# Weights' second parts by an adding DMA, four sets of parts, no parts kept in DRAM

## The chip, the cores and the metric

The kernel runs on one core of a Trainium2 chip. The metric is the device time of one execution in microseconds (us); the median of three runs before is 2469.33 us. Five engines work in parallel, each through its own queue in order: TensorE (PE, its weight loads PEld), VectorE (DVE), ScalarE (ACT), GpSimd (POOL) and SyncE (SP, which here only issues DMAs). POOL issues DMAs too; the transfers of all of them run on the core's 16 DMA engines.

## What is computed

One encoder layer over two sequences of 1024 tokens by 1024 channels. Each sequence is normalised and projected with w_in (1024 by 8192). A Fourier branch, a two-step long convolution (Hyena) branch and their gates follow; each branch is projected by a 1024 by 1024 matrix, they are merged by sigmoid gates, projected once more, normalised and added to the input.

```python
xn = rmsnorm(x, g_pre)
p = xn @ w_in
fv, fg, hv, hg, mg = jnp.split(p, [...], axis=-1)
fz = jnp.fft.fftn(fz, axes=(1, 3), norm="ortho").real
y_f = (fz * jax.nn.silu(fg)) @ w_fourier_out
...
for n, gate in enumerate((x1, x2)):
    z = gate * long_conv(z, kf[:, n], hyena_d[n])
y_h = (z * jax.nn.silu(hg)) @ w_hyena_out
g_f, g_h = jnp.split(jax.nn.sigmoid(mg + b_merge), 2, axis=-1)
out = (g_f * y_f + g_h * y_h) @ w_out
return x + rmsnorm(out, g_post)
```

All is float32. TensorE is fed with a rounded type (F32R), so each operand is held as two parts: the rounded value h, and the rest l = value - h. A product takes three matmuls (h by h, h by l, l by h).

## The kernel before

The stages, by their place in the span: Fourier branch of both sequences (to about 700 us; from some 200 us on, the filters of the convolutions and most gate sections of the first sequence are worked in between), convolutions of the first sequence (about 760 to 1145) and of the second (1145 to 1710), the rest of the second sequence's gate sections (to 1960, most of it in a form that has its own weights' parts), the output projections `phase_out` (1960 to 2306) and the last projection `last_rows` (to the end). The order on each engine is made when the kernel is built, by a scheduler that estimates durations.

A weight tile [128, 1024] is used in two halves [128, 512], 256 KB each. What becomes of a half:

- `inproj` (line 714) makes the input projections: SP loads the raw half wr (line 729), ACT rounds it into wh (line 171), POOL subtracts, wl = wr - wh (line 181). There are two buffers each of wr, wh and wl. In the convolutions of the first sequence POOL also stores both parts in DRAM (d_w, line 733), and for the second sequence SP loads the two parts from there (line 726), with no rounding and no subtraction. A half feeds 24 matmuls: 4 blocks of 128 rows, 2 halves of the sequence, 3 products.
- `weight` inside `phase_out` (line 1106) does it for the output projections: POOL loads the raw half (line 1113), ACT rounds, DVE subtracts. There are three sets: two in the pool wp, and every third half has one of its own in the pool op. A half feeds 12 matmuls, as each unit of work has half a sequence. There are 4 units, 2 matrices, 8 output tiles and 2 halves: 128 halves. For each output tile a 256 KB gate g is loaded (line 1141), passed through a sigmoid on ACT (line 1143) and multiplied in by DVE; the next unit's operands (sf, sh) are loaded and split meanwhile (lines 1099 and 1103).
- `phase_gates` and `last_rows` take the same two tags wh and wl for two of their parts, split by ACT and DVE.

`split` (line 168) writes h by ACT or DVE and l by POOL or DVE. A tile's buffers are taken in turn; whoever writes a buffer waits until its last reader is done.

Of the kernel before, what the change touches and what calls it, by code (L numbers as in the profile page):

```python
# [9 lines left out]
F32 = mybir.dt.float32  # L10
F32R = mybir.dt.float32r
# [3 lines left out]
MUL, ADD, SUB = ALU.mult, ALU.add, ALU.subtract  # L15

P = 128
D = 1024
L = 1024
# [142 lines left out]
class K:  # L162
# [5 lines left out]
    def split(self, h, l, src, eng="pool", heng="act"):  # L168
# [4 lines left out]
            nc.vector.tensor_copy(h, src)  # L173
        self.left = self.sub(eng, l, src, h)

    def stt(self, eng, out, a, s, b, op0=MUL, op1=ADD):
        self.nc.vector.scalar_tensor_tensor(out, a, s, b, op0=op0, op1=op1)  # L177

# [18 lines left out]
    def setup(self, ctx):  # L197
        tc, nc, a = self.tc, self.nc, self.a
        self.cp = cp = ctx.enter_context(tc.tile_pool(name="cp", bufs=1))
        self.ps = ctx.enter_context(tc.tile_pool(name="ps", bufs=2, space=bass.MemoryType.PSUM))  # L200
        self.dr = ctx.enter_context(tc.tile_pool(name="dr", bufs=1, space=bass.MemoryType.DRAM))

        def ld(name, shape, src, eng=nc.sync):
            t = cp.tile(shape, F32, name=name)
            eng.dma_start(t, src)
            return t
        self.ident = ld("ident", [P, P], a["c_id"], nc.gpsimd)
        self.gpre = ld("gpre", [P, 8], a["g_pre"], nc.gpsimd)
# [12 lines left out]
        self.d_h1 = dt("d_h1", [P, L])  # L221
        self.d_x = [[dt(f"d_x{b}_{k}", [P, L]) for k in range(8)] for b in range(NB)]
        self.d_fz = [[dt(f"d_fz{b}_{k}", [P, L]) for k in range(8)] for b in range(NB)]
        self.d_k = [[dt(f"d_k{n}_{c}", [P, 32 * P]) for c in range(8)] for n in range(2)]
        self.d_g = [{s: [dt(f"d_g{b}_{s}_{k}", [P, L]) for k in range(8)] for s in (0, 4, 5, 6)} for b in range(NB)]
        self.d_w = [[[dt(f"d_w{s}_{k}_{i}", [P, L]) for i in range(2)] for k in range(8)] for s in range(3)]
        self.d_m = [dt(f"d_m{u}", [P, 4, 8, P]) for u in range(2 * NB)]
        self.d_t = [dt(f"d_t{j}", [P, 4, 512]) for j in range(2)]
        self.d_sh = [[dt(f"d_sh{b}_{k}", [P, L]) for k in range(8)] for b in range(NB)]
# [481 lines left out]
            self.xh.append(h)  # L711
            self.xl.append(l)

    def inproj(self, sec, mt, b=None):

        nc, a = self.nc, self.a
        ps = [self.psum("mm", 4, f"pin{n}") for n in range(2)]
        for q in range(2):
            s = slice(512 * q, 512 * q + 512)
            h = self.wp.tile([P, 4, P], F32R, tag="wh", name="wh", bufs=2)  # L720
            l = self.wp.tile([P, 4, P], F32R, tag="wl", name="wl", bufs=2)
            parts = [t.rearrange("p a b -> p (a b)") for t in (h, l)]
            kept = self.d_w[sec - 1][mt] if b is not None else None
            if b:
                for t, k in zip(parts, kept):
                    nc.sync.dma_start(t.bitcast(F32), k[:, s])
            else:
                r = self.wp.tile([P, 512], F32, tag="w", name="wr", bufs=2)
                nc.sync.dma_start(r, a["w_in"][sec, mt][:, s])
                self.split(*parts, r, "pool", "act")  # L730
                if kept:
                    for t, k in zip(parts, kept):
                        nc.gpsimd.dma_start(k[:, s], t.bitcast(F32))
            for n in range(2):
                for kk in range(4):
                    k = 4 * q + kk
                    s = slice(512 * n, 512 * n + 512)
                    self.mm3(ps[n], (h[:, kk], l[:, kk]), (self.xh[k][:, s], self.xl[k][:, s]), k == 0, k == 7)
        return ps

    def conv(self, sec, ct, ws, name, b):
        nc = self.nc
        ps = self.inproj(sec, ct, b)
        out = ws.tile([P, L], F32, tag="u" if sec == 1 else "x", name=name, bufs=1 if sec == 1 else 4)
        w = lambda j: self.wsh[:, ((sec - 1) * 8 + ct) * 3 + j:((sec - 1) * 8 + ct) * 3 + j + 1]
        H = 512
        for n in range(2):
            nc.scalar.activation(out[:, H * n:H * n + H], ps[n], AF.Copy, scale=w(1))
        for o, n, r in ((1, 0, slice(0, H)), (H + 1, 1, slice(0, H - 1))):
            o = out[:, o:o + r.stop]  # L750
            self.stt("dve", o, ps[n][:, r], w(0), o)
        for o, n, r in ((0, 0, slice(1, H)), (H - 1, 1, slice(0, H))):
            o = out[:, o:o + r.stop - r.start]
            self.stt("dve", o, ps[n][:, r], w(2), o)
        return out
# [215 lines left out]
    def phase_gates(self):  # L971
# [3 lines left out]
        tc, nc, a = self.tc, self.nc, self.a  # L975
        wp, b = self.wp, 1
        jobs = [(s, c) for c in range(0, 8, 2) for s in (0, 4, 5, 6) if (s, c) not in self.PLAIN]
        with ExitStack() as es:
            pool = lambda n: es.enter_context(tc.tile_pool(name=n, bufs=1, reuse_waits="tile"))
            gs, gw, gr = pool("gs"), pool("gw"), pool("gr")  # L980
            def prepare(sec, c):


                r = gr.tile([P, 4, 512], F32, tag="raw", name="wraw", bufs=2)
                for i in range(2):
                    nc.gpsimd.dma_start(r[:, 2 * i:2 * i + 2].rearrange("p a b -> p (a b)"), a["w_in"][sec, c + i])
                s = gw.tile([P, 4, 512], F32, tag="sum", name="wsum", bufs=1)
                A = {}

                def parts(n, pool, tags, src, bufs):  # L990
                    h, l = [pool.tile([P, 4, P], F32R, tag=t, name=t, bufs=bufs) for t in tags]
                    self.split(h.rearrange("p a b -> p (a b)"), l.rearrange("p a b -> p (a b)"), src, "dve", "act")
                    A[n] = h, l
                parts("11", wp, ("wh", "wl"), r[:, 0], 2)
                parts("12", wp, ("wh", "wl"), r[:, 1], 2)
# [86 lines left out]
    def phase_out(self):  # L1082
# [6 lines left out]
        with ExitStack() as es:  # L1089
            pool = lambda n: es.enter_context(tc.tile_pool(name=n, bufs=1, reuse_waits="tile"))  # L1090
            bl, sp, oc, sc, op = pool("bl"), pool("sp"), pool("oc"), pool("sc"), pool("op")
            self.nw = 0

            def operand(i, nm, k):

# [10 lines left out]
            def weight(w, dt, q):  # L1106


                own = self.nw % 3 == 2
                self.nw += 1  # L1110
                pool, nb = (op, 1) if own else (wp, 2)
                r = pool.tile([P, 512], F32, tag="w", name="wr", bufs=nb)
                nc.gpsimd.dma_start(r, a[w][dt][:, 512 * q:512 * q + 512])  # L1113
                h = pool.tile([P, 4, P], F32R, tag="wh", name="wh", bufs=nb)
                l = pool.tile([P, 4, P], F32R, tag="wl", name="wl", bufs=nb)
                self.split(h.rearrange("p a b -> p (a b)"), l.rearrange("p a b -> p (a b)"), r, "dve", "act")
                self.weighed, self.weighed2 = self.rounded, self.left
                return h, l

# [118 lines left out]
    def last_rows(self, units, B11, B21, B22, T1, T2, T3, T4, gp, op):  # L1238
# [6 lines left out]
        def prepare(i):  # L1245
# [14 lines left out]
            for n, r, pool, nb in (("11", r0, op, 1), ("12", r1, wp, 2)):  # L1260
                parts(n, r, *[pool.tile([P, 4, P], F32R, tag=t, name=t, bufs=nb) for t in ("wh", "wl")])
# [176 lines left out]
```

## Time and profile before

| what | value |
|---|---|
| three runs, us | 2466.95, 2469.33, 2469.89 |
| span of the profiled execution, us (first to last instruction) | 2468.1 |
| mean granted TensorE clock | 0.994 |
| moved by DMA | 429.39 MB, 174 GB/s in the mean |
| raw halves loaded for the input projections | 136, median 3.1 us to landing |
| raw halves loaded for the output projections | 64 + 64, median 3.9 and 3.8 us to landing |
| parts stored in DRAM, and loaded again | 96 stores (4.0 and 4.9 us), 96 loads (2.9 and 3.7 us) |

The page and the traces give times from the start of the span. Busy times are sums over instructions of one engine; "idle before" is how long that engine stood still ahead of the group, with the releaser that ended most of it. A DMA's time to landing runs from its issue. The DMA share is the mean busy share of the 16 DMA engines. For the profiled execution the page gives the span alone; the median of the runs is 1.2 us above it.

### The profile page before, as it was taken

What the parts mean: (1) busy time and instruction counts of PE and PEld (TensorE: products, weight loads), DVE (VectorE), ACT (ScalarE), POOL (GpSimd) and SP (SyncE); (2) the same over time, 40 slices, a digit from 0 to 9 for tenths busy, and PEclk for the clock granted to TensorE, in tenths of its full rate; (3) what the DMA queues carried; (4) which work ended last, traced back from release to release, by engine and by line L of the source; (5) the groups of instructions that cost most, each with busy time, mean ns of one, the idle gap of its engine ahead of it and who ended that gap; (6) DMA issues with size and microseconds to landing.
All of it is one profiled execution on the core that took longest, in us unless ns stands there. A gap on an engine that the chain in (4) does not pass through costs nothing.

```text
span 2468.1 us, 37202 instructions
## 1 busy us (share of the span) xinstructions
PE 2408.3 (98%) x13196; PEld 2090.7 (85%) x13196; DVE 1947.5 (79%) x3725; ACT 1093.3 (44%) x2041; POOL 498.2 (20%) x516
## 2 busy tenths in 40 slices
PE   6999999999989999999999999999999999999998
PEld 6988888888878988888889888888788888888886
DVE  7687788888888999999889999985565455665677
ACT  5546666666654333334223222333343444544443
POOL 1331222212234333442000000112200012112121
PEclk9999999999999999999999999999999999999999
DMA  7535544444556455545443443435445567776543
GB/s 272 180 128 210 206 163 151 156 160 156 169 184 201 161 176 175 162 161 199 137 145 129 137 144 131 136 129 175 154 162 173 196 201 267 246 244 221 165 168 128
DMA packets 225155, 429.39 MB, mean 174 GB/s; under 512 B 23542, under 2 KB 87255, under 8 KB 224456
## 3 DMA queue, kind: packets, MB, share of 16 engines
q1 hardware_dynamic: 198444, 333.34, 40.6%
q0 software_dynamic: 26336, 93.65, 10.8%
q8 instruction: 104, 1.70, 0.3%
q14 instruction: 83, 0.68, 0.1%
q10 hardware_dynamic: 188, 0.02, 0.0%
HBM read 290.60 MB, written 136.31 MB: 173 GB/s over the span
## 4 chain that ended last, share of the span: by engine, by line
PE 55%; DMA 2%; issue 1%; DVE 1%; POOL 0%; ACT 0%; DVEq 0%; SPq 0%; ACTq 0%; POOLq 0%
PE pin L194 20%; PE pg L194 8%; PE po L194 6%; PE pT L194 6%; PE pyh L194 5%; PE pX L194 5%; PE pyf L194 5%; DMA wr<-in_w_fo 1%; PE tph L785 1%; DMA g<-d_g 1%; DMA wr<-in_w_ho 0%; DVE wl L181 0%; POOL wr L1113 0%; ACT wh L171 0%; POOL wl L181 0%
## 5 line engine op out<-in xcount | busy, mean ns | idle before, releaser
L194 PE MATMUL pin<-xh,wh 128*128 128x512 f32 x1472 | 578.2, 394 | 4.3 <-DVE v L177 2.9
L194 PE MATMUL pin<-xh,wl 128*128 128x512 f32 x1472 | 577.1, 393 | 2.5 <-POOL wl L181 2.5
L194 PE MATMUL pin<-xl,wh 128*128 128x512 f32 x1472 | 578.4, 393 | 0.0
L181 POOL TENSOR_TENSOR wl<-wr,wh 128x512 fp32r<-128x512 f32 x136 | 253.5, 1865 | 1162.8 <-ACT wh L171 1120.3
L194 PEld LDWEIGHTS pin<-xh,wh 128*128 128x128 f32 x1472 | 278.4, 189 | 55.6 <-DVE v L177 3.1
L194 PEld LDWEIGHTS pin<-xh,wl 128*128 128x128 f32 x1472 | 278.3, 189 | 54.0 <-POOL wl L181 3.4
L194 PEld LDWEIGHTS pin<-xl,wh 128*128 128x128 f32 x1472 | 278.5, 189 | 51.5 <-DVE xl L181 0.4
L171 ACT CAST wh<-wr 128x512 fp32r<-128x512 f32 x264 | 162.7, 618 | 304.3 <-PE pin L194 106.8
L194 PE MATMUL pT<-cinv,yh 128*128 128x256 f32 x1024 | 192.1, 282 | 0.0
L194 PEld LDWEIGHTS pT<-cinv,yh 128*128 128x128 f32 x1024 | 164.8, 190 | 9.5 <-ACT yh L171 0.2
L181 DVE TENSOR_TENSOR t<-pX,k 128x1024 f32<-128x1024 f32 x128 | 155.4, 1214 | 9.7 <-PE pX L194 8.7
L181 DVE TENSOR_TENSOR wl<-wr,wh 128x512 fp32r<-128x512 f32 x128 | 87.1, 687 | 92.6 <-ACT wh L171 92.3
L194 PE MATMUL pX<-bh,cfwd 128*128 128x256 f32 x768 | 160.1, 287 | 0.0
L194 PE MATMUL pyf<-sf,wh 128*128 128x512 f32 x512 | 157.7, 389 | 0.0
L194 PE MATMUL pyh<-sh,wh 128*128 128x512 f32 x512 | 157.2, 389 | 0.0
L171 ACT CAST yh<-y 128x512 fp32r<-128x512 f32 x128 | 79.5, 621 | 153.7 <-DVE y L181 120.6
L194 PE MATMUL pT<-cinv,yl 128*128 128x256 f32 x512 | 144.9, 283 | 1.2 <-DVE yl L181 1.2
L171 ACT CAST bh<-b 128x512 fp32r<-128x512 f32 x144 | 88.6, 619 | 119.9 <-DVE b L181 81.5
L181 DVE TENSOR_TENSOR bl<-b,bh 128x512 fp32r<-128x512 f32 x144 | 110.6, 769 | 23.4 <-ACT bh L171 23.4
L194 PEld LDWEIGHTS pX<-bh,cfwd 128*128 128x128 f32 x768 | 125.5, 190 | 3.0
L194 PEld LDWEIGHTS pyf<-sf,wh 128*128 128x128 f32 x512 | 96.0, 188 | 20.3 <-ACT wh L171 0.5
L194 PEld LDWEIGHTS pyh<-sh,wh 128*128 128x128 f32 x512 | 96.1, 188 | 20.0
(350 smaller groups left out, 5322.9 us busy)
## 6 DMA issues: line engine op xcount, KB each, us to landing
k<-d_k SPq DMA_DIRECT2D x128, 512.0 KB, 4.0
wr<-in_w_in SPq DMA_DIRECT2D x136, 256.0 KB, 3.1
d_g<-gt SPq DMA_DIRECT2D x124, 256.0 KB, 2.5
d_k<-kt SPq DMA_DIRECT2D x128, 128.0 KB, 2.2
d_k<-kt SPq DMA_DIRECT2D x64, 256.0 KB, 2.3
wr<-in_w_fo POOLq DMA_DIRECT2D x64, 256.0 KB, 3.9
g<-d_g SPq DMA_DIRECT2D x64, 256.0 KB, 3.8
wr<-in_w_ho POOLq DMA_DIRECT2D x64, 256.0 KB, 3.8
```

The costliest lines, as they stand in the source:

```text
L171: self.rounded = nc.scalar.copy(h, src)
L181: return e.tensor_tensor(out, a, b, op=op)
L194: return self.nc.tensor.matmul(out, lhsT, rhs, start=start, stop=stop, skip_group_check=shared)
L785: nc.tensor.transpose(tp[:, q * P:(q + 1) * P], eo[:, e, q], self.ident)
```

## The change

A new helper makes the two parts. ACT rounds the raw half into h, ACT writes -h into l, and a DMA issued from POOL adds the raw half to l, read from DRAM a second time, where the addition is made by the transfer itself. `inproj` uses it for every half of both sequences, and nothing is stored in d_w or loaded from it; `weight` uses it in the output projections. The tags wh and wl have four buffers in wp, the raw half two; the third set in op is gone. `phase_gates` and `last_rows` keep their own way of splitting and take the four buffers. The memory that the kernel reserves for descriptors of POOL's DMAs is set to 8192.

```diff
+    def parts(self, h, l, r, src):
+
+        nc = self.nc
+        self.rounded = nc.scalar.copy(h, r)
+        nc.scalar.mul(l, h, -1.0)
+        self.left = nc.gpsimd.dma_start(l, src, accum_op=ADD)
...
-    def inproj(self, sec, mt, b=None):
+    def inproj(self, sec, mt):
...
-            h = self.wp.tile([P, 4, P], F32R, tag="wh", name="wh", bufs=2)
-            l = self.wp.tile([P, 4, P], F32R, tag="wl", name="wl", bufs=2)
-            parts = [t.rearrange("p a b -> p (a b)") for t in (h, l)]
-            kept = self.d_w[sec - 1][mt] if b is not None else None
-            if b:
-                for t, k in zip(parts, kept):
-                    nc.sync.dma_start(t.bitcast(F32), k[:, s])
-            else:
-                r = self.wp.tile([P, 512], F32, tag="w", name="wr", bufs=2)
-                nc.sync.dma_start(r, a["w_in"][sec, mt][:, s])
-                self.split(*parts, r, "pool", "act")
-                if kept:
-                    for t, k in zip(parts, kept):
-                        nc.gpsimd.dma_start(k[:, s], t.bitcast(F32))
+            h = self.wp.tile([P, 4, P], F32R, tag="wh", name="wh", bufs=4)
+            l = self.wp.tile([P, 4, P], F32R, tag="wl", name="wl", bufs=4)
+            r = self.wp.tile([P, 512], F32, tag="w", name="wr", bufs=2)
+            src = a["w_in"][sec, mt][:, s]
+            nc.sync.dma_start(r, src)
+            self.parts(*[t.rearrange("p a b -> p (a b)") for t in (h, l)], r, src)
...
-                own = self.nw % 3 == 2
-                self.nw += 1
-                pool, nb = (op, 1) if own else (wp, 2)
-                r = pool.tile([P, 512], F32, tag="w", name="wr", bufs=nb)
-                nc.gpsimd.dma_start(r, a[w][dt][:, 512 * q:512 * q + 512])
-                h = pool.tile([P, 4, P], F32R, tag="wh", name="wh", bufs=nb)
-                l = pool.tile([P, 4, P], F32R, tag="wl", name="wl", bufs=nb)
-                self.split(h.rearrange("p a b -> p (a b)"), l.rearrange("p a b -> p (a b)"), r, "dve", "act")
+                r = wp.tile([P, 512], F32, tag="w", name="wr", bufs=2)
+                src = a[w][dt][:, 512 * q:512 * q + 512]
+                nc.gpsimd.dma_start(r, src)
+                h = wp.tile([P, 4, P], F32R, tag="wh", name="wh", bufs=4)
+                l = wp.tile([P, 4, P], F32R, tag="wl", name="wl", bufs=4)
+                self.parts(h.rearrange("p a b -> p (a b)"), l.rearrange("p a b -> p (a b)"), r, src)
...
-    nc = bacc.Bacc("TRN2", target_bir_lowering=False, num_devices=1)
+    nc = bacc.Bacc("TRN2", target_bir_lowering=False, num_devices=1, dynamic_dma_scratch_size=8192)
```

The order on the engines is new nearly everywhere in detail. Two places carry it. On POOL, in the output projections, before (wr is a raw half; POOL has nothing but these loads there):

```order
L1113 DMA wr_21582<-in_w_ho 128x512
L1113 DMA wr_21611<-in_w_ho 128x512
L1113 DMA wr_21629<-in_w_ho 128x512
L1113 DMA wr_21658<-in_w_ho 128x512
L1113 DMA wr_21676<-in_w_ho 128x512
```

Each load waits for a free buffer, three halves back. The same place with the change (L1108 is the raw load, L181 the adding DMA into wl; the raw half of wl_21505 is wr_21502, and so on, 3 lower):

```order
L181 DMA wl_21505<-in_w_ho 128x512
L1108 DMA wr_21579<-in_w_ho 128x512
L181 DMA wl_21533<-in_w_ho 128x512
L1108 DMA wr_21598<-in_w_ho 128x512
L181 DMA wl_21552<-in_w_ho 128x512
L1108 DMA wr_21628<-in_w_ho 128x512
```

Loads and adding DMAs now alternate: the raw load of the half after the next stands just ahead of a half's adding DMA. On ACT at that place, before (g is the gate with its sigmoid, sf and sh the next unit's operands):

```order
L171 CAST wh_21613<-wr_21611 128x512
L171 CAST wh_21631<-wr_21629 128x512
L171 CAST sf5_21602<-sf5_21602 128x512
L1143 ACTIVATE g_21651<-g_21651,bm_70 128x512
L171 CAST wh_21660<-wr_21658 128x512
L171 CAST wh_21678<-wr_21676 128x512
```

and with the change (L179 rounds, L180 writes the negated part):

```order
L179 CAST wh_21504<-wr_21502 128x512
L1138 ACTIVATE g_21523<-g_21523,bm_70 128x512
L180 ACTIVATE wl_21505<-wh_21504 128x512
L179 CAST wh_21532<-wr_21530 128x512
L180 ACTIVATE wl_21533<-wh_21532 128x512
L179 CAST wh_21551<-wr_21549 128x512
L171 CAST sf0_21521<-sf0_21521 128x512
L1138 ACTIVATE g_21572<-g_21572,bm_70 128x512
L180 ACTIVATE wl_21552<-wh_21551 128x512
```

Each rounding has its negation behind it, for every second half with a gate's sigmoid in between.

More of the change, by code (lines that the diff above doesn't have):

```diff
@@ L225, in setup @@
         self.d_g = [{s: [dt(f"d_g{b}_{s}_{k}", [P, L]) for k in range(8)] for s in (0, 4, 5, 6)} for b in range(NB)]
-        self.d_w = [[[dt(f"d_w{s}_{k}_{i}", [P, L]) for i in range(2)] for k in range(8)] for s in range(3)]
         self.d_m = [dt(f"d_m{u}", [P, 4, 8, P]) for u in range(2 * NB)]
@@ L742, in conv @@
         nc = self.nc
-        ps = self.inproj(sec, ct, b)
+        ps = self.inproj(sec, ct)
         out = ws.tile([P, L], F32, tag="u" if sec == 1 else "x", name=name, bufs=1 if sec == 1 else 4)
@@ L993, in parts @@
                     A[n] = h, l
-                parts("11", wp, ("wh", "wl"), r[:, 0], 2)
-                parts("12", wp, ("wh", "wl"), r[:, 1], 2)
+                parts("11", wp, ("wh", "wl"), r[:, 0], 4)
+                parts("12", wp, ("wh", "wl"), r[:, 1], 4)
                 self.add("dve", s[:, 0:2], r[:, 2].unsqueeze(1).to_broadcast([P, 2, 512]), r[:, 3::-3])
@@ L1091, in phase_out @@
             bl, sp, oc, sc, op = pool("bl"), pool("sp"), pool("oc"), pool("sc"), pool("op")
-            self.nw = 0
             def operand(i, nm, k):
@@ L1259, in xpair @@
                 return t[:, 0], t[:, 1]
-            for n, r, pool, nb in (("11", r0, op, 1), ("12", r1, wp, 2)):
-                parts(n, r, *[pool.tile([P, 4, P], F32R, tag=t, name=t, bufs=nb) for t in ("wh", "wl")])
+            for n, r in (("11", r0), ("12", r1)):
+                parts(n, r, *[wp.tile([P, 4, P], F32R, tag=t, name=t, bufs=4) for t in ("wh", "wl")])
             s13 = xp.tile([P, 2, 512], F32, tag="xl3", name="ms13", bufs=1)
```

## The prediction

> **What bounds the kernel now.** I read the engines' shares first, then windows stage by stage, then who waits for whom, then the DMA queues. The shares and slices of the page:
>
> ```profile
> PE 2408.3 (98%) x13196; PEld 2090.7 (85%) x13196; DVE 1947.5 (79%) x3725; ACT 1093.3 (44%) x2041; POOL 498.2 (20%) x516
> ```
>
> TensorE is the bound, with 2468.1 - 2408.3 = 59.8 us without a matmul in the span. The windows (us from the span's start; length; busy us of PE, PEld, DVE, ACT, POOL; granted clock; DMA share; GB/s) say where:
>
> ```profile
> 200.00:300.00 100.00, 97.26 (x543) 84.60 (x542) 71.49 (x148) 61.22 (x121) 23.51 (x22) 0.98 0.65 233
> 300.00:500.00 200.00, 194.61 (x1046) 168.06 (x1045) 163.36 (x391) 131.82 (x289) 43.72 (x25) 0.98 0.48 156
> 500.00:700.00 200.00, 195.13 (x1038) 167.67 (x1036) 166.47 (x387) 126.33 (x275) 44.17 (x33) 0.99 0.51 165
> 700.00:760.00 60.00, 54.44 (x287) 46.70 (x288) 52.94 (x117) 27.58 (x58) 19.64 (x22) 0.94 0.58 189
> 760.00:1145.00 385.00, 383.84 (x2311) 342.01 (x2311) 372.95 (x642) 140.89 (x237) 148.76 (x131) 1.00 0.50 167
> 1145.00:1645.00 500.00, 500.00 (x2982) 444.21 (x2981) 455.36 (x835) 152.69 (x253) 24.28 (x10) 1.00 0.43 146
> 1710.00:1766.00 56.00, 54.26 (x239) 44.51 (x239) 36.43 (x37) 21.18 (x28) 19.45 (x15) 1.00 0.64 225
> 1960.00:2306.00 346.00, 345.50 (x1522) 284.88 (x1521) 203.76 (x312) 161.41 (x266) 67.31 (x126) 1.00 0.70 235
> ```
>
> From 760 on TensorE hardly stops. The output projections (1960 to 2306) lose 0.5 us, and there the DMA engines are busiest: 0.70 of their time. TensorE's pace stands in the chain of waits (start, us, what):
>
> ```profile
> 1709.97 43.11 PE pin L194 x190
> 1999.90 43.52 PE pyh L194 x192
> ```
>
> A matmul takes 43.52 / 192 = 0.227 us. A weight half feeds 24 matmuls in the input projections (5.44 us) but only 12 in the output projections: **2.72 us** for each of their 128 halves.
>
> **The change, part by part.**
>
> *Subtractions leave POOL and DVE.* Their rows, and the one for DVE's same-shaped split in the convolutions:
>
> ```profile
> L181 POOL TENSOR_TENSOR wl<-wr,wh 128x512 fp32r<-128x512 f32 x136 | 253.5, 1865 | 1162.8 <-ACT wh L171 1120.3 <-PE pft L194 14.5 <-PE pXf L194 10.3
> L181 DVE TENSOR_TENSOR wl<-wr,wh 128x512 fp32r<-128x512 f32 x124 | 84.4, 686 | 80.6 <-ACT wh L171 80.3
> PE pin L194 <- POOL wl L181: 2.5, 2, 1.7
> PE pyh L194 <- DVE wl L181: 0.5, 1, 0.5
> ```
>
> POOL loses 253.5 us and DVE 128 x 0.686 = 88 us, but TensorE waited 2.5 + 0.5 = 3.0 us for them in the whole span. That is all these can give directly: -3 us.
>
> *ACT gains 312 negations* (136 + 48 + 128) and 48 roundings that the second sequence used to skip. The nearest row for a scaled copy of this shape, SBUF to SBUF, is the first; the others stand around it in the output projections:
>
> ```profile
> L1034 ACT ACTIVATE gt<-gt 128x512 f32<-128x512 f32 x24 | 14.9, 633 | 3.5 <-DVE gt L181 3.5
> L171 ACT CAST wh<-wr 128x512 fp32r<-128x512 f32 x124 | 76.4, 620 | 138.1 <-PE pyh L194 46.9 <-PE pyf L194 44.8 <-DMA wr<-in_w_fo 26.9
> L1143 ACT ACTIVATE g<-g,bm 128x512 f32<-128x512 f32 x64 | 46.1, 722 | 39.5 <-DMA g<-d_g 35.8 <-DVE sh L181 2.1 <-DVE wl L181 0.9
> L171 ACT CAST sh<-sh 128x512 fp32r<-128x512 f32 x31 | 19.0, 614 | 0.0
> L1113 POOL DMA_DIRECT2D wr<-in_w_fo x57 | 30.6, 536 | 128.7 <-DVE wl L181 127.7 <-DMA wr<-in_w_fo 0.7
> ```
>
> 312 x 0.633 + 48 x 0.620 = 227 us on an engine that is busy 1093 of 2468. In the output projections 161.4 + 128 x 0.633 = 242 of 346 us: ACT fits, so 0 us, hidden by TensorE's 2.72 us per half; without that cover it would be 128 x 0.633 = 81 us there.
>
> *312 adding DMAs come, 96 stores to DRAM and 96 loads from it go, 48 weight loads come.* In the convolutions of the first sequence (760 to 1145) two stores per half go and one adding DMA comes; in the second (1145 to 1645) two loads become a load and an adding DMA, 48 halves in 500 us at a share of 0.43, which even at two passes grows by 48 x 0.78 / 500 = 0.07. TensorE has 5.44 us per half there, other matmuls in between, and four sets in place of two. I cost these at 0: the matmuls before them hide the landing, and were they gone each half would cost the 5 us or so of one. The eight gate halves in a row at 1710 to 1766 add 8 x 2 x 0.78 = 12.5 us to the 36 us of work that the engines have in those 56 (the 0.78 is worked out below): room enough, and I allow 3 us, twice what TensorE misses there now. What decides is the output projections. Their queues and landings:
>
> ```profile
> q1 hardware_dynamic: 36093, 47.30, 40.6%
> q0 software_dynamic: 10192, 33.56, 28.9%
> DMA to landing us min/median/max: 2.8/3.8/7.7
> d_w<-wl POOLq DMA_DIRECT2D x48, 256.0 KB, 4.9
> 2120.00:2140.00 20.00, 20.00 (x90) 16.57 (x89) 11.85 (x19) 9.11 (x16) 4.31 (x9) 1.00 0.95 320
> ```
>
> POOL's queue q0 moved 33.56 MB, which is 128 transfers of 256 KB, in 28.9% of 346 us = 100 us of all 16 engines: 0.78 us for each. With q1, the engines are busy 0.695 x 346 = 240.5 us (the two queues of instructions add 1 us). Now 128 adding transfers of the same size come on top. No row shows one. Below, an adding transfer costs the engines what a plain load costs, 0.78 us: 241.5 + 100 = 341.5 us of work in a 346 us stage. It would fit with nothing to spare; the fullest window shown reaches 0.95, so 341.5 / 0.95 = 359 us, +13. Above, it costs two passes, as 256 KB stored and then loaded again does: 241.5 + 200 = 441.5 us, so the stage is **+95 us**, and 441.5 / 0.95 = 465 us, +119, if 0.95 is all they reach. I take two passes: the addition needs the 256 KB of weights and the 256 KB that already lie in the tile, so the same engines have twice the bytes to read.
>
> The Trainium skill (Collectives: The Full Stack, section "The bandwidth ceiling: the fold count and why AG ≠ RS ≠ AR") says the same of another program: a DMA that adds is slower than a copy because of its two source reads, both on the read ring, and it gives a measured ratio of 1.93. By that, as an estimate, the stage would be 88 us longer in place of 95; no run here shows it yet.
>
> *The order* on ACT and POOL there, as it is shown with the change: the raw load of half n+2 is asked for just ahead of the adding DMA of half n. Every second negation stands behind a sigmoid that itself waits for the transfer of g (35.8 us in all before), and the adding DMA and the next raw load wait behind it on POOL. A set is free when TensorE ends half n-4 and needed three halves, 8.16 us, later. On the way: 0.62 + 0.61 + 0.72 + 0.63 us on ACT and 0.54 us on POOL, 3.1 us; so the adding DMA may take 5.0 us to land. A store lands in 4.9, a load and a store in turn 3.8 + 4.9 = 8.7. At 8.7 a set goes round in 3.1 + 8.7 + 2.72 = 14.5 us, 3.63 a half: 128 x 0.91 = +116 us. This is the same wait seen from another side, not a second term: full engines make late landings.
>
> Sum: 2468.1 - 3 + 3 + 95 = 2563 us of span. The median of the runs shown, 2469.33, lies 1.2 us above this execution's span: **2564 us**.
>
> **The rivals.**
>
> *Cheap addition.* An adding transfer costs about one load, 0.78 us. For it: a plain 256 KB transfer also reads and writes, and the tile's old content lies in SBUF, not in DRAM. Against it: even so the stage needs 341.5 of 346 us. +13, up to +40 if landings pass 5.0 us in the full windows: 2482 to 2509.
>
> *Latency, not bytes.* The raw halves had three buffers and have two. A buffer comes round in its landing plus the rounding, and two halves last 5.44 us, so a raw load may take 5.44 - 0.62 = 4.8 us. Today's median is 3.8, but the chain of waits shows loads of
>
> ```profile
> 2132.11 6.21 DMA wr<-in_w_fo
> 2218.07 7.54 DMA wr<-in_w_fo
> ```
>
> At 7.7, the slowest, a half takes (7.7 + 0.62) / 2 = 4.16 us: 128 x 1.44 = +184, so 2653. Its mark is a DMA share well below 0.95 while ACT waits for wr.
>
> *Not slower: the engines hide it and DVE runs freer.* If the adding costs no more than a load and the four sets ride over the full windows, the output projections stay at 346 us, and what is left is relief from 200 to 760, where TensorE lacks 2.7 + 5.4 + 4.9 + 5.6 = 18.6 us. For it: DVE's subtraction of one shape takes longer beside POOL's work,
>
> ```profile
> L181 DVE TENSOR_TENSOR bl<-b,bh 128x512 fp32r<-128x512 f32 x144 | 110.6, 769 | 23.4 <-ACT bh L171 23.4
> ```
>
> 769 ns against 686 where POOL computes nothing. Half of the 18.6 us would be -9: 2460. It decides from the point where an adding transfer costs under 0.8 us of the engines and lands within 5.0 us. Against it: ACT, busiest just there (61 to 66%), gets the negations of 60 gate halves before 760, 38 us.
>
> *Not what it says.* The adding DMA may be cut into far smaller pieces than a row. At four times a load's price, 3.1 us, the output projections alone need 241.5 + 400 us, +295, and the input projections fill too: above 2760.
>
> **How the numbers follow.** Two passes 46%, latency 16%, cheap addition 17%, not slower 17%, small pieces 4%. The forecast is that of two passes, 2564; its own range is 2524 (1.6 passes, 241.5 + 160 us) to 2588 (two passes at 0.95). The range for 8 in 10 reaches from 2475, below the cheap addition's time, to 2655, the slowest latency. What a measurement of this kernel tells from no change is about 0.2%, 5 us. The -9 us rival gives faster 10% and, with only part of the relief, the same 7%; the rest, 83%, is slower.
>
> **What would show it.** Right: in the output projections the DMA share goes to 0.9 or more, the stage lasts about 440 us, TensorE waits there for wl from DMA, and everything up to 1960 starts within 10 us of today. A share near 0.7 to 0.8 with a longer stage is the latency rival; a stage of 346 us at any share makes the prediction wrong; so would a loss that lies in the convolutions, where I cost the change at nothing because the sets are ready long before 5.44 us are over.

## The result

The changed kernel takes 2605.64 us (median of 4 runs, 2595.78 to 2610.54) against 2468.14 (4 runs, 2466.22 to 2469.89): 1.0556 times the time before, with a 95% interval of 1.0532 to 1.058. The profiled run took 2608.23 us, its span is 2606.5: 138.4 us more than the 2468.1 before. The page's first part, in the order of the one before:

```profile
PE 2453.9 (94%) x13196; PEld 2102.0 (81%) x13196; DVE 1816.1 (70%) x3597; ACT 1285.3 (49%) x2394; POOL 482.1 (18%) x596
```

TensorE now lacks 152.6 us of its span, before 59.8. So 92.8 of the 138.4 us are time without a matmul; in the other 45.6 the same 13196 matmuls took longer (2453.9 us busy in place of 2408.3). The windows of the changed kernel (same columns; the bounds of the later ones are shifted with the program):

```profile
200.00:300.00 100.00, 93.32 (x473) 79.31 (x472) 38.53 (x79) 47.97 (x92) 14.64 (x22) 0.95 0.80 243
300.00:500.00 200.00, 197.40 (x1072) 170.31 (x1072) 156.37 (x402) 145.02 (x319) 24.01 (x28) 1.00 0.74 197
500.00:700.00 200.00, 192.84 (x1036) 166.11 (x1035) 150.92 (x391) 139.82 (x305) 22.48 (x26) 0.99 0.72 191
700.00:780.00 80.00, 60.99 (x311) 52.63 (x310) 68.28 (x168) 39.94 (x86) 3.46 (x4) 0.81 0.44 128
780.00:1165.00 385.00, 385.00 (x2326) 343.47 (x2325) 361.57 (x650) 164.72 (x281) 68.32 (x56) 1.00 0.55 145
1165.00:1665.00 500.00, 500.00 (x2977) 444.13 (x2976) 455.04 (x839) 210.39 (x356) 52.80 (x58) 1.00 0.57 149
1728.00:1784.00 56.00, 56.00 (x253) 46.55 (x252) 32.89 (x38) 25.82 (x36) 9.37 (x13) 1.00 0.81 243
1971.00:2444.00 473.00, 392.57 (x1550) 297.69 (x1549) 136.81 (x191) 234.92 (x394) 181.81 (x253) 0.95 0.94 246
```

Two stages lost time. The output projections last 473 us in place of 353 and keep the DMA engines busy for 0.94 of it; TensorE's matmuls there take 392.57 us, about 40 more than before, at a granted clock of 0.95 in place of 1.00. Ahead of the convolutions, from 700 to 780, TensorE lacks 19 us. The convolutions (780 to 1665) and the eight gate halves (1728 to 1784) run without a gap.

To compare kernels I take three marks from the views of single tiles: the first matmul of the gates (pg<-xh,wh), the first of the output projections (pyf<-sf,wh) and the start of their last (pyh<-sh,wl). In the rows (count, ns of one, first and last start) they are 1765.8, 1953.5 and 2305.7 us before, and 1783.8, 1971.5 and 2444.1 after:

```profile
L194 PE MATMUL pg<-xh,wh x80: 389/389/389, 1765.8 to 1936.5; 128*128 128x512 f32 x80
L194 PE MATMUL pyf<-sf,wh x512: 388/389/497, 1953.5 to 2262.0; 128*128 128x512 f32 x171
L194 PE MATMUL pyh<-sh,wl x256: 389/389/500, 2000.2 to 2305.7; 128*128 128x512 f32 x128
...
L201 PE MATMUL pg<-xh,wh x80: 389/389/389, 1783.8 to 1954.5; 128*128 128x512 f32 x80
L201 PE MATMUL pyf<-sf,wh x512: 387/389/794, 1971.5 to 2388.8; 128*128 128x512 f32 x171
L201 PE MATMUL pyh<-sh,wl x256: 387/389/740, 2032.9 to 2444.1; 128*128 128x512 f32 x128
```

So 18.0 us are lost ahead of the gates, 120.4 in the output projections (472.6 against 352.2 us) and nothing behind them: 18.0 + 120.4 = 138.4.

Who waits for whom in the output projections of the changed kernel (engine, tile, releaser; total us, times, longest), for TensorE and then for ACT:

```profile
PE pyh L201 <- DMA wl<-in_w_ho: 26.6, 28, 3.6
PE pyf L201 <- DMA wl<-in_w_fo: 25.0, 20, 3.3
PE pyf L201 <- ACT wh L179: 19.1, 10, 5.6
PE pyh L201 <- ACT wh L179: 9.2, 3, 5.2
...
ACT wh L179 <- DMA wr<-in_w_ho: 70.2, 43, 3.9
ACT wh L179 <- DMA wr<-in_w_fo: 69.4, 37, 4.1
ACT g L1138 <- DMA g<-d_g: 62.7, 19, 8.4
```

TensorE waits 51.6 us for adding DMAs and 28.3 us for roundings; ACT waits 139.6 us for raw halves. Most of these waits are for transfers. Their queues in that window (packets, MB, share of 16 engines), and the median landings over the span:

```profile
q0 software_dynamic: 28507, 67.17, 63.1%
q1 hardware_dynamic: 37043, 48.91, 31.0%
...
wr<-in_w_fo POOLq DMA_DIRECT2D x64, 256.0 KB, 5.9
wl<-in_w_fo POOLq DMA_DIRECT2D x64, 256.0 KB, 6.7
```

POOL's queue moved 67.17 MB, as much as 256 transfers of 256 KB (a few of them belong to the last projection), in 63.1% of 473 us = 298 us. If 128 plain ones cost 0.78 us each as before, 198 us are left for 128 adding ones: about 1.55 us each, twice a load. A raw half now lands in 5.9 us, before in 3.8.

### The profile page after: what moved, and what is told of

It is laid out like the page before. It is cut to its first block, busy times and chain, and to the rows that moved or that the text cites. A ratio compares the mean times of both kernels' runs of the same rounds, so it can differ in the third digit from the quotient of the medians.

```text
span 2606.5 us, 37627 instructions
## 1 busy us (share of the span) xinstructions
PE 2453.9 (94%) x13196; PEld 2102.0 (81%) x13196; DVE 1816.1 (70%) x3597; ACT 1285.3 (49%) x2394; POOL 482.1 (18%) x596
## 4 chain that ended last, share of the span: by engine, by line
PE 70%; DMA 14%; issue 7%; DVE 4%; POOL 2%; ACT 2%; SPq 0%; POOLq 0%; DVEq 0%; ACTq 0%
PE pin L201 36%; PE pT L201 7%; PE pX L201 6%; PE pg L201 6%; PE po L201 6%; DMA wr<-in_w_fo 5%; DMA wr<-in_w_ho 4%; PE pXf L201 2%; PE pfv L201 2%; POOL wl L181 1%; PE tph L783 1%; DMA d_g<-gt 1%; POOL wr L1108 1%; PE pft L201 1%; DMA g<-d_g 1%
## 5 line engine op out<-in xcount | busy, mean ns | idle before, releaser
L181 POOL DMA_DIRECT2D wl<-in_w_in x184 | 160.5, 874 | 1321.6 <-ACT wl L180 1097.7
L179 ACT CAST wh<-wr 128x512 fp32r<-128x512 f32 x312 | 193.1, 619 | 419.6 <-PE pin L201 245.0
L180 ACT ACTIVATE wl<-wh 128x512 fp32r<-128x512 f32 x312 | 195.6, 628 | 5.3 <-issue 1.2
L201 PE MATMUL pyf<-sf,wh 128*128 128x512 f32 x512 | 166.5, 412 | 19.1 <-ACT wh L179 19.1
L201 PE MATMUL pyh<-sh,wl 128*128 128x512 f32 x256 | 104.9, 416 | 26.9 <-DMA wl<-in_w_ho 26.6
L201 PE MATMUL pyf<-sf,wl 128*128 128x512 f32 x256 | 106.3, 420 | 25.2 <-DMA wl<-in_w_fo 25.0
```

The costliest lines, as they stand in the source:

```text
L179: self.rounded = nc.scalar.copy(h, r)
L180: nc.scalar.mul(l, h, -1.0)
L181: self.left = nc.gpsimd.dma_start(l, src, accum_op=ADD)
L201: return self.nc.tensor.matmul(out, lhsT, rhs, start=start, stop=stop, skip_group_check=shared)
```

## Experiments

Times without an interval are single profiled runs; the kernel before ran beside them (medians 2467.66 to 2470.48). Stage means the time between the second and third mark.

**The price by itself.** No layer is computed; 48 transfers of 256 KB of each kind, eight buffers in turn:

```diff
+        for i in range(N):
+            nc.gpsimd.dma_start(T[i % 8], src(i))
+        for i in range(N):
+            nc.gpsimd.dma_start(T[i % 8], src(i), accum_op=ADD)
+        for i in range(N):
+            nc.gpsimd.dma_start(T[i % 8], S[i % 8], accum_op=ADD)
+        for i in range(N):
+            nc.sync.dma_start(T[i % 8].bitcast(F32), src(i))
```

> A small kernel that computes nothing of the layer: 48 transfers of 256 KB each of four kinds, eight in flight at a time: plain loads issued from POOL, adding transfers with the weights read from DRAM, adding transfers with the weights read from SBUF, plain loads issued from SP; then the outputs are written. Two-pass theory: a plain load takes 0.75 to 0.8 us of all engines each (48 in 36 to 38 us), an adding one 1.5 to 1.6 (72 to 77 us), the same from SBUF 1.5 or a little less. One-pass theory: adding and plain ones take the same, 36 to 40 us for 48. Small-pieces theory: over 2.5 us each, 120 us or more for 48.

The slices of the page (GB/s in 40 parts of 229 us), then the DMA issues on POOL (busy us, mean ns): adding from SBUF, adding from DRAM, plain.

```profile
GB/s 151 352 391 383 386 385 377 269 205 204 205 204 205 204 204 205 204 204 205 204 204 196 192 189 184 184 184 184 185 192 252 295 398 386 393 404 406 405 406 238
...
L1418 POOL DMA_DIRECT2D t<-s x48 | 41.4, 866 | 25.9 <-DMA t<-s 22.3
L1416 POOL DMA_DIRECT2D t<-in_w_in x48 | 41.8, 1020 | 15.0 <-DMA t<-in_w_in 14.5
L1414 POOL DMA_DIRECT2D t<-in_w_in x48 | 25.6, 541 | 12.7 <-DMA t<-in_w_in 7.0
```

Plain loads run at about 385 GB/s, 262 KB in 0.68 us; adding ones at 204 GB/s, 1.28 us. Both prices are below what was expected; their ratio, 385 / 204.5 = 1.88, is that of two passes. The Trainium skill (Collectives: The Full Stack, "The bandwidth ceiling: the fold count and why AG ≠ RS ≠ AR") has 1.93 for another program, the rate of a collective that copies over that of one that adds, and puts it down to two source reads; this run is near it. The ratio alone does not tell which of the bytes are counted twice.

Three windows of the same run (length, busy us of POOL, granted clock, DMA share, GB/s), of plain loads from POOL, of adding ones from DRAM, and of plain loads from SP:

```profile
10.00:36.00 26.00, 18.20 (x35) 1.00 1.26 385
55.00:92.00 37.00, 24.96 (x29) 1.00 1.13 204
180.00:195.00 15.00, 0.00 (x0) 1.00 1.03 382
```

The share adds up the times of packets, and goes above 1 here. So a share of 0.9 or more in the kernel does not by itself show that the engines could take no more.

**The output projections taken apart.** First, DVE splits there as before, all else as in the change (four sets, two raw buffers):

```diff
-                self.parts(h.rearrange("p a b -> p (a b)"), l.rearrange("p a b -> p (a b)"), r, src)
+                self.split(h.rearrange("p a b -> p (a b)"), l.rearrange("p a b -> p (a b)"), r, "dve", "act")
```

> The changed kernel with the output projections' second parts made by DVE again (four sets, two raw buffers kept), the input projections' by adding DMAs. If the adding transfers' bytes hold up the output projections: that stage falls back to 346 to 350 us and the time to 2486 (2468 + 18, the loss ahead of it, which stays). If two raw buffers in place of three do it: the stage stays above 400 us and the time above 2540.

2518.91 us, ratio 1.0212 (1.019 to 1.0234): the stage takes 377.8 us, 25.6 more than before, with no adding DMA in it. That lies between the two times expected. Its window, and what ACT waits for there:

```profile
1969.90:2347.50 377.60, 362.42 (x1547) 289.97 (x1546) 206.86 (x315) 162.52 (x267) 68.14 (x127) 0.99 0.67 219
...
ACT wh L171 <- DMA wr<-in_w_ho: 104.3, 51, 7.4
ACT wh L171 <- DMA wr<-in_w_fo: 74.9, 45, 5.1
```

The engines are at 0.67 while ACT waits 179 us for raw halves. This is the mark that the prediction gave for its rival "latency, not bytes". Five raw buffers in place of two test it, with DVE's splits and with the adding DMAs:

```diff
+                own = self.nw % 5 > 1
+                self.nw += 1
-                r = wp.tile([P, 512], F32, tag="w", name="wr", bufs=2)
+                r = op.tile([P, 512], F32, tag="wraw", name="wr", bufs=3) if own else wp.tile([P, 512], F32, tag="w", name="wr", bufs=2)
```

> As e1_out_dve (DVE splits in the output projections, four sets), with five raw buffers there in place of two. If e1's 26 us in the output projections were the two raw buffers, the stage from the first pyf to the last pyh matmul falls from 378 to 352 us and the time from 2519 to 2485 to 2493. If they were something else of the four sets' order, it stays at 375.

> The changed kernel with five raw buffers in place of two in the output projections, adding DMAs kept. Two-pass theory: nothing to gain, the stage stays within 10 us of the changed kernel's (about 466 us), the time 2595 to 2612, DMA share 0.95. Latency theory: ACT no longer waits for raw halves, the stage falls by 40 us or more, the time to 2565 or less.

With DVE's splits: 2487.86 us, the stage 352.3 us, as before. So the 25.6 us came from the raw buffers (two here, three before, five now). With the adding DMAs: 2599.49 us, the stage 461.6, only 11.0 less than the change. The two raw buffers are a real limit, but one that the adding DMAs mostly cover. Then, still with five raw buffers and all halves added, SP issues the raw loads, so that POOL's queue holds adding DMAs alone:

```diff
-                nc.gpsimd.dma_start(r, src)
+                nc.sync.dma_start(r, src)
```

> All 128 halves added, five raw buffers, raw loads issued by SP. If bytes bound the stage (441.5 us of engine work by two passes), the order of issue does not matter and the stage stays at 445 to 465 us (461.4 with POOL issuing) at a share of 0.94 to 0.98. If the order on POOL's queue were the bound, it falls below 435 us, which two passes do not allow.

2581.25 us, the stage 441.2 us, and the DMA share is the highest of all these kernels (window, then the queues in it):

```profile
1975.40:2417.40 442.00, 387.61 (x1552) 301.60 (x1551) 134.62 (x190) 231.41 (x391) 110.99 (x129) 0.94 0.98 260
...
q1 hardware_dynamic: 54213, 80.26, 54.1%
q0 software_dynamic: 18432, 34.35, 43.6%
```

Issuing the raw loads from SP was worth 20.4 us (it changes the order and the queue at once), which "the order of issue does not matter" had not allowed; but below 435 us it does not go either, and 0.98 of 442 us is 433 us of packets' time. That the engines could take no more is not shown by this: at the rates of the run of transfers alone the window's bytes would take, as an estimate, 121 x 1.28 us for the adding ones and 83.2 MB / 385 GB/s for the rest, 371 of the 442 us. The queues give both prices in the kernel itself. On q1, 80.26 MB are 306 plain transfers in 0.541 x 442 = 239 us: 0.78 us each. On q0, 34.35 MB are 131 transfers, ten of them plain (five loads of 512 KB of the last projection); 0.436 x 442 - 10 x 0.78 = 185 us for 121 adding transfers: **1.53 us each, 1.96 times a plain one**.

Half as many adding DMAs (DVE splits every second half), five raw buffers, the raw loads once from POOL and once from SP (the line that both have):

```diff
-                self.parts(h.rearrange("p a b -> p (a b)"), l.rearrange("p a b -> p (a b)"), r, src)
+                (self.split(h.rearrange("p a b -> p (a b)"), l.rearrange("p a b -> p (a b)"), r, "dve", "act") if q else
+                 self.parts(h.rearrange("p a b -> p (a b)"), l.rearrange("p a b -> p (a b)"), r, src))
```

> Five raw buffers in the output projections, and there every second half is split by DVE, every other by an adding DMA: 64 adding DMAs in place of 128. Bytes theory: the engines have 247 + 64 x 1.55 = 346 us of work; at 0.94 the stage lasts 352 to 370 us, time 2488 to 2506. If a fixed cost of the mechanism (the order on POOL, the late landings) decides, half of the 109 us of e4 stays: 405 us and 2540.

> As the half-adding kernel with five raw buffers (stage 412 us at a DMA share of 0.85), but the raw loads are issued by SP, so that POOL's queue holds the adding DMAs alone. If the 60 us there came of adding DMAs that stand behind raw loads on POOL, the stage falls to 352 to 375 us at a share of 0.93 or more. If they came of the adding DMA's own landing behind ACT's rounding and negation (5.6 us in the median), or of engines that are already full in bursts, it stays at 400 to 420 us.

2545.58 and 2532.07 us, stages 412.2 and 399.1 us. The windows of the two, and TensorE's waits in the second:

```profile
1969.00:2381.00 412.00, 369.67 (x1548) 296.37 (x1547) 167.66 (x254) 200.75 (x329) 122.77 (x185) 0.97 0.85 239
```

```profile
1968.00:2368.00 400.00, 366.33 (x1553) 295.68 (x1552) 167.13 (x254) 201.36 (x329) 56.90 (x67) 0.97 0.87 246
...
PE pyf L201 <- DMA wl<-in_w_fo: 17.5, 8, 4.1
PE pyh L201 <- DMA wl<-in_w_ho: 15.3, 9, 4.0
```

Bytes alone would give 241.5 + 64 x 1.56 = 341 us of work, which fits into 352. The stage is 47 us longer all the same, at a share of 0.87. So by the terms set for the first of these two runs the bytes lost (352 to 370 us) and the fixed cost of the mechanism won (405 us). Half the adding DMAs leave 60.0 of 109.4 us with POOL issuing the raw loads, and 46.9 of 89.0 with SP: 0.73 us for each added half, against 0.70 with all of them added. A limit of the engines over the stage as a whole, which 64 added halves stay below, would have left next to nothing. What these runs show is a price per added half, and not a point at which the engines fill; the issue from POOL explains 13 us of it.

TensorE waits 32.8 us for the added halves and the granted clock is 0.97. The trace of the second kernel shows in part what holds them up. One case (start, us, instruction, idle time before it and its releaser):

```profile
2183.60 0.72 ACT L1142 ACTIVATE g<-g,bm 128x512 f32<-128x512 f32 x1 [4.47 <-DMA g<-d_g]
2186.93 0.72 ACT L1142 ACTIVATE g<-g,bm 128x512 f32<-128x512 f32 x1 [1.57 <-DMA g<-d_g]
2189.01 0.61 ACT L179 CAST wh<-wr 128x512 fp32r<-128x512 f32 x1
2189.66 0.63 ACT L180 ACTIVATE wl<-wh 128x512 fp32r<-128x512 f32 x1
2190.59 0.88 POOL L181 DMA_DIRECT2D wl<-in_w_fo  x1 [10.29 <-ACT wl L180]
2195.95 0.50 PE L201 MATMUL pyf<-sf,wl 128*128 128x512 f32 x1 [4.06 <-DMA wl<-in_w_fo]
```

ACT stands at two sigmoids until their gates land, then rounds and negates the next half, and its adding DMA lands 5.3 us after its issue, 4.06 us too late. TensorE waits 17 times for an added half here. In 14 of them ACT had waited for a gate between the negation before and the half's own (of all 64 negations, 29 are of this kind); in the other three the adding DMA took 7.6 to 9.6 us to land (median of all 5.8). No run takes the sigmoids out of ACT's way, or gives the added halves more than four sets, so the gates, the landing, the number of sets and engines that are full for a few us at a time are not separated.

The adding DMA replaced by a plain one to the same place, with everything else as in the change, two raw buffers included (wl then holds the raw weights, not the rest):

```diff
-        self.left = nc.gpsimd.dma_start(l, src, accum_op=ADD)
+        self.left = nc.gpsimd.dma_start(l, src) if plain else nc.gpsimd.dma_start(l, src, accum_op=ADD)
```

> The changed kernel with the output projections' adding DMA replaced by a plain DMA of the same 256 KB into the same tile, at the same place in the queues (the second parts are then the raw weights: the product is wrong by that). Every wait, buffer and queue is as in the changed kernel, only the addition is gone. Two-pass theory: the engines have 241.5 + 100 us of work, the stage takes 350 to 375 us and the time is 2490 to 2515. Latency theory (order on POOL, two raw buffers): the stage stays above 420 us and the time above 2560.

2556.26 us, the stage 418.4 us, just under what the latency theory had (above 420) and far from the 350 to 375 of two passes:

```profile
1974.00:2392.00 418.00, 375.42 (x1547) 297.15 (x1546) 136.65 (x191) 234.29 (x393) 135.43 (x253) 0.96 0.88 278
```

So even a second plain transfer in the same place would have cost this stage 66 us (the raw buffers alone made 25.6 with DVE's splits); the addition itself costs 472.6 - 418.4 = 54 us more, in place of the 100 us that its second pass has in the prediction. The plain transfer with five raw buffers and SP's loads was not run, so how much of the 89 us there belongs to the addition is open.

**Ahead of the output projections.** The kernel before, unchanged in how it makes its parts, but with four sets in wp, two raw buffers and the change's descriptor memory (the diff is against the kernel before, its part in the input projections):

```diff
-            h = self.wp.tile([P, 4, P], F32R, tag="wh", name="wh", bufs=2)
-            l = self.wp.tile([P, 4, P], F32R, tag="wl", name="wl", bufs=2)
+            h = self.wp.tile([P, 4, P], F32R, tag="wh", name="wh", bufs=4)
+            l = self.wp.tile([P, 4, P], F32R, tag="wl", name="wl", bufs=4)
```

> The kernel before, splits and stored parts as they were, with only the memory of the change: four sets in wp (none in op), two raw buffers, 8192 for descriptors. If the 18 us ahead of 1960 come from where the four sets lie in memory (the filters' first load, hidr, is then issued some 100 us late in SP's queue), they are here too: the first pX matmul at 770 us in place of 751, and with the output projections' 26 us that e1 showed the time is 2505 to 2520. If they come from the adding DMAs, pX starts at 751 and the time is 2490 to 2496.

2534.45 us. The gates start at 1796.2 us, 30.4 later than before and 12.4 later than with the change: the loss is there, and larger, without a single adding DMA. (The rest is in the output projections: 386.0 us, 33.8 more than before, again with two raw buffers.) What the traces show late in both is the load of the filters' hidden layer, hidr. Its rows before and with the change (the last times are those of the issue on SP):

```profile
L870 SPq DMA_DIRECT2D hidr<-d_h x1: 326/326/326, 204.6 to 204.6; - x1
```

```profile
L868 SPq DMA_DIRECT2D hidr<-d_h x1: 423/423/423, 263.8 to 263.8; - x1
```

In the kernel of this experiment it is issued at 260.2 us. The descriptor memory is not the reason: the next two kernels have it too, and issue this load early. Until the load lands, the filters' work on DVE and ACT cannot start: DVE is busy 38.53 us of 200 to 300, before 71.49. TensorE does gate sections meanwhile; from 700 to 780 it stands still for 19 us. Next, adding DMAs in all input projections but two sets, so that no tile moves, and the output projections as before (the diff is against the change, its part in the input projections):

```diff
-            h = self.wp.tile([P, 4, P], F32R, tag="wh", name="wh", bufs=4)
-            l = self.wp.tile([P, 4, P], F32R, tag="wl", name="wl", bufs=4)
+            h = self.wp.tile([P, 4, P], F32R, tag="wh", name="wh", bufs=2)
+            l = self.wp.tile([P, 4, P], F32R, tag="wl", name="wl", bufs=2)
```

> Adding DMAs in all input projections, but with two sets of parts as before, so that no tile moves in memory; the output projections as before (DVE subtracts, three sets). Theory A (the 18 us lost ahead of 1960 belong to the four sets' memory, and the adding itself costs the input projections nothing): the filters' hidden layer is loaded at about 204 us again, the Fourier branch ends at 712 to 742 us in place of 763, the convolutions of the first sequence start at or before 751 us, the output projections last 352 us, and the whole 2440 to 2470 us. Theory B (the four sets were what hid the adding): with two sets a half's chain (0.62 + 0.63 us on ACT, 0.5 on POOL, 5.0 to land = 6.8 us) has to fit beside one half's 5.44 us of matmuls; up to 1.4 us is lost at each of the 128 halves of the convolutions' projections that no other matmul covers, so the convolutions lengthen by 50 to 180 us: 2510 to 2640 us, with TensorE waiting there for wl from DMA.

2511.37 us, ratio 1.0172 (1.0159 to 1.0186). hidr is early (201.7 us), and still the gates start 34.6 us later than before, at 1800.4. A new first row stands in TensorE's waits over the whole span:

```profile
PE pin L201 <- DMA wl<-in_w_in: 35.6, 24, 4.8
```

Theory B has the wait right, but not its place and size: 19.2 of the 35.6 us fall between 200 and 700, where the gate sections are, and 7.9 between 700 and 1710, where it had the convolutions lengthen by 50 to 180. That the time lies at the low end of its range is luck. The changed kernel has no such row, so four sets do hide the adding there. Then two of the four sets in another pool (wb), the output projections as before:

```diff
+            room = self.rooms[self.ni % len(self.rooms)]
+            self.ni += 1
-            h = self.wp.tile([P, 4, P], F32R, tag="wh", name="wh", bufs=4)
-            l = self.wp.tile([P, 4, P], F32R, tag="wl", name="wl", bufs=4)
+            h = room.tile([P, 4, P], F32R, tag="wh", name="wh", bufs=2)
+            l = room.tile([P, 4, P], F32R, tag="wl", name="wl", bufs=2)
```

> Adding DMAs in all input projections, four sets there, of which two lie in wp and two in the convolutions' own pool, so that hidr is issued as early as before; output projections split by DVE with three sets and three raw buffers, as in the kernel before; 8192 for descriptors. If adding DMAs in the input projections cost TensorE nothing and free DVE and POOL, the filters end 5 to 15 us earlier: 2452 to 2464. If the 18 us come from the adding DMAs after all: 2480 to 2488.

2504.28 us, ratio 1.0143 (1.0126 to 1.016). hidr is issued at 203.4 us again and the Fourier branch's last matmul pXf starts at 711.4 us, before at 742.0; but the gates start at 1764.6, only 1.2 us early, and then lose some 32 us, since their sums are no longer prepared ahead (the first, xsum, at 1773.1 us, before at 1730.3):

```profile
1764.00:1800.00 36.00, 13.88 (x33) 8.27 (x33) 26.29 (x28) 13.19 (x14) 1.66 (x4) 0.59 0.45 160
```

Last, the kernel with DVE's splits and five raw buffers (2487.86 us), with one line changed: one pool opens ahead of another, which gives hidr other memory.

```diff
-            mf, wa, wb, mi = pool("mf"), pool("wa"), pool("wb"), pool("mi")
+            wa, mf, wb, mi = pool("wa"), pool("mf"), pool("wb"), pool("mi")
```

> As the kernel with DVE's splits and five raw buffers in the output projections (2487.86 us; adding DMAs and four sets in the input projections), with one line changed: of the four pools of the main stage, wa is opened ahead of mf, so that the filters' hidden layer hidr lies in other memory and is the seventh DMA of its group on SP, as before, in place of the thirtieth. Theory A (the 18 us ahead of 1960 come from memory that the four sets push about, which makes hidr late): hidr is issued at about 205 us, the Fourier branch ends at 711 to 742 us, the gates start at 1760 to 1767 us, the output projections last 352 us, the whole 2460 to 2472 us: what the adding DMAs save DVE and POOL then shows as at most 8 us. Theory B (the adding DMAs crowd the transfers between 200 and 760 us, whatever hidr does): hidr early, but the gates start at 1775 us or later, the whole 2480 to 2490 us.

2476.93 us, ratio 1.0031 (1.0018 to 1.0044). hidr's row, and the first matmul of the gates:

```profile
L868 SPq DMA_DIRECT2D hidr<-d_h x1: 327/327/327, 202.7 to 202.7; - x1
...
L201 PE MATMUL pg<-xh,wh x80: 389/389/389, 1766.6 to 1938.9; 128*128 128x512 f32 x80
```

The gates start 0.8 us later than before, in place of 15.0 for that kernel without the line. Theory A holds for where the loss comes from: tiles that the four sets moved in memory, and hidr is the one whose load the traces show late. (The line moves the other tiles of the two pools as well.) The total is 5 us above its range, and the relief it allowed for did not come. This is the best version with adding DMAs that ran; it is still slower than the kernel before, by 8.4 us of span: 3.6 by the start of the output projections and 4.8 in them, which no run explains.

## Why the prediction was right, and where it was not

- **The price of an adding transfer, and the place where it is paid: right.** It was taken at 2 x 0.78 = 1.56 us and measured at 1.53 in the kernel, 1.28 against 0.68 alone. The output projections have 120.4 of the 138.4 us.
- **That full engines set the time there: not shown.** Predicted were 441.5 us of work; the changed kernel's window has 0.94 x 473 = 445 us of packets' time, the one with the highest share 433. But 64 added halves, which leave the engines at 0.87, cost 46.9 us, and 128 cost 89.0. In these two kernels the loss goes with the number of adding DMAs, also where their bytes leave room.
- **The stage: +95 predicted, +120.4 measured.** The step that fails is "the same wait seen from another side, not a second term: full engines make late landings". Late landings come without full engines: at a share of 0.87 the adding DMAs still take 5.8 us (median), where the prediction allows 5.0. By the prediction's own sum for a set's round, the 6.7 us to landing of the row above give 3.1 + 6.7 + 2.72 = 12.5 us, 3.13 a half and, as an estimate, +52 us, with no wait for a gate in it. By the experiments 89.0 us remain with five raw buffers and a queue of its own for the adding DMAs (441.2 - 352.2), 20.4 us came from raw loads and adding DMAs together on POOL, 11.0 from two raw buffers. The three parts come from kernels changed one after the other; in another order they would share out differently, as 25.6 against 11.0 us for the raw buffers shows. So +95 against 89.0, and the +119 with engines at 0.95 against 120.4, are near for a reason that the runs do not bear out, and in that part luck. The measured 2605.64 us lie above the range of the two-pass theory itself (2524 to 2588), inside the range for 8 in 10.
- **"Everything up to 1960 starts within 10 us of today": wrong, 18.0 us.** The 18 us stand at nothing in the sum. The prediction asked what waits for added halves, and not what four sets in wp do to the memory of other tiles. One load then stood some 25 places later on SP, 59 us later in time. It did not follow hidr, whose issue the build's order would have shown.
- **Convolutions and gate halves at nothing: right, for the reason given.** TensorE is busy 385.00 of 385, 500.00 of 500 and 56.00 of 56 us there, with the engines at 0.55, 0.57 and 0.81. With two sets the cover was gone and 35.6 us appeared. The 3 us allowed for the gate halves and the 3 us credited for subtractions both came to about nothing.
- **ACT hidden: only half shown.** 312 negations took 195.6 us (628 ns each, 633 taken), and ACT was not full (234.92 of 473 us). But ACT's order is not free: in the second half-adding kernel 14 of TensorE's 17 waits for an added half have a wait of ACT for a gate ahead of them. How much time that costs was not measured by a run.
- **The rivals.** *Latency* was real: 25.6 us alone for the raw buffers, not the 184 that every load at its slowest would make, and some part of the 89.0 us that no run tells. *Cheap addition* would not have saved the kernel as it is: with a plain second load the stage still grew by 66 us, where the prediction had 13 to 40. *Not slower*: DVE did run freer (the 144 subtractions of the row that the prediction shows, bl<-b,bh, take 709 ns in place of 769; the Fourier branch is 30.6 us earlier with two sets in wb), but the convolutions behind it began only 5.6 us earlier, the gates 1.2, and no version came out faster for it. *Small pieces* fell with the first experiment.

The median came out 41.6 us above the 2564 forecast: 18.0 ahead of the stage and 120.4 - 95 = 25.4 in it, less some 2 us, since this median lies 0.9 us below the profiled execution's span, where the forecast had put it about 1 above.

## What to carry to other kernels

Work moved from an engine into an adding DMA is paid for with two transfers' worth of DMA time, so count it against the fullest stage and not the mean share. Then do not stop at the bytes: here each added half cost the stage about 0.7 us, whether 64 or 128 were added and the share was 0.87 or 0.98. Follow the chain of one half, with what stands ahead of it on each engine, its landing and the number of sets, as a term of its own, and halve the number of transfers to see whether a limit of the bytes is there at all. And when a tag gets more buffers, look for what moved in memory: here one small load, far from the change, cost 18 us, and the order in which two pools are opened gave most of it back.

## What the runs showed of the hardware

- Adding from a tile in SBUF is slower than from DRAM: 184 against 204 GB/s with eight buffers in turn. So reading the source from DRAM is not what limits an adding transfer here.
- POOL is busy 0.87 to 1.02 us with the issue of an adding DMA and 0.54 with a plain one's, in the run of transfers alone, where the row of the prediction for plain loads has 536 ns.
- Plain 256 KB loads reach 382 to 385 GB/s over the windows shown with eight tiles in turn (the 405 at the end of the slices are stores of results, in part beside loads), but the same load takes 0.78 us of packets' time of all engines in the kernel (336 GB/s), beside other traffic.
- The DMA share can go above 1: 1.26, 1.13 and 1.03 in the windows of the run of transfers alone.
- Where TensorE waits, the granted clock is lower as well: 0.81 granted in the window 700 to 780 where it lacks 19 us, and 0.94 to 0.97 through the output projections in the windows shown with 34 to 80 us without a matmul, against 1.00 before.
